# A diffusion layer on one core: gate projections as 32-column strips, context work behind the loop over x

## The chip, the cores and the metric

The kernel runs on one core of one Trainium2 chip. The metric is device microseconds of one execution; the kernel before is given by the median of three runs. A second source is one profiled execution, whose instructions were recorded by the hardware profiler. Its engines are TensorE (PE, with its weight loads shown apart as PEld), VectorE (DVE), ScalarE (ACT), GpSimd (POOL) and SyncE (SP), which issues every DMA of this kernel.

## The reference, cut to what matters

One layer of a diffusion backbone: 512 latent tokens `x` and 256 context tokens `ctx`, both 1024 wide, in fp32.

```
mod  = silu(c) @ w_ada + b_ada            # shift and scale, one value per channel; mod_c the same from c_ctx
h    = rms_norm(x, g)   * (1 + scale)   + shift
hc   = rms_norm(ctx, g) * (1 + scale_c) + shift_c
aq, ak, av, dq, dk, dv, dz, da, db, ga, gd = split(h @ w_in)     # da, db: 16 columns each
caq, cak, ...                              = split(hc @ w_in)
beta = sigmoid(db);  g = -exp(a_log) * softplus(da + dt_bias)    # gates of the delta recurrence
...                                       # attention, delta recurrence, branch projections, MLP
```

The change concerns only the way from `x`, `ctx` and `c` to `h`, `hc`, the first projections (`dk` among them) and the gates `da`, `db`.

## The kernel before

All activations lie channel by channel: the 1024 channels are eight row tiles (`kt`, 0 to 7) of 128 partitions, and tokens are columns, 512 of `x` beside 256 of `ctx`. A projection tile is 128 columns of `w_in`, multiplied for each `kt`. To keep fp32 precision with faster products, weights and activations are split into a high and a low part (`wload`, L240 on ACT for the high part, L241 on DVE for the low one), and `mm3` adds three products for each `kt`: high with high (L289), high with low (L290), low with high (L291). The gates `da` and `db` fill a projection tile of their own, `T_AB`, of whose 128 columns 32 hold weights and the rest zeros.

The start of the kernel, the part that changes, runs as follows.

- 36 products of a constant (L188) run on PE while the first transfers come in.
- The mean square: ACT squares `x` in four pieces (L265), DVE adds the pieces and folds them (L269, L273), one product with a matrix of ones sums over the channels (L276), and ACT takes logarithm and exponential (L146), which gives `rx`. The same follows for the context and gives `rc`.
- Modulation: for each `kt`, `ada(kt)` multiplies the condition vectors with 1 MB of `w_ada`, in two transfers of 512 KB. Its eight products per `kt` (L207) are strips: each writes 32 of the 128 rows of the result, four strips side by side. `columns(kt)` copies the result out (L221, ACT), turns it into columns with two narrow products (L226, PE), and DVE makes the scale column (L229) and the shift column (L230).
- The loop over `kt`: `modulate` gives `h`: DVE multiplies by scale and `rx` (L294), ACT adds the shift and rounds to the high part (L295), DVE forms the low part (L296). It does so for 512 columns of `x` and 256 of the context. `ada` and `columns` of `kt + 2` follow (`AHEAD`), and then `mm3` of three tiles whose weights were loaded early (`EARLY`): `T_AB`, `T_DK` and `T_DK + 1`.
- Then come `T_DK + 2` and `T_DK + 3`, whose weights pass through a queue (`wq`, `wnext`), the gates' element work (L608 to L622), and L649, the first products that use the gates.

Every engine works through its instructions in a fixed order, which the framework's scheduler sets when the program is built, so that the order of the source is not the order of the program: rows of both are shown with the change.

## Time and profile before

| | us |
|---|---|
| median of 3 runs (939.95 to 941.4) | 940.95 |
| span of the profiled execution, first to last instruction | 938.6 |
| PE busy in the span | 907.7 (97%) |
| PE weight loads | 732.9 (78%) |
| DVE busy | 596.5 (64%) |
| ACT busy | 444.2 (47%) |

The span lies 2.35 us under the median of the runs; the profiled execution has no other time of its own. A matmul shows as two entries where its operands are plain fp32. Busy time of PE counts overlapping matmuls once, and the length of a matmul holds its way through the array: matmuls in a dense row follow each other faster than each of them lasts.

### The profile page before, as it was taken

Reading aid. Unit: us, or ns where it says so; the run is one execution under the profiler, and the core shown is the slowest. Engines: PE = TensorE matmul, PEld = TensorE weight load, DVE = VectorE, ACT = ScalarE, POOL = GpSimd, SP = SyncE. Lnnn points to the kernel's source line nnn. Section 1 sums busy time; section 2 is a strip of 40 time slices with the busy share of each in tenths; the row PEclk is TensorE's granted clock in tenths of the full one; section 3 lists DMA queues with packets and bytes.
Section 4 is the critical chain, followed back from the end, with each engine's and each line's share of the span. In section 5 each row is a group of like instructions: output and inputs, shape, how many; then the busy total and the mean of one; then the engine's idle time right before and its main releaser. Section 6 shows DMA issues by size and latency. Waiting matters only on the chain.

```text
span 938.6 us, 18221 instructions
## 1 busy us (share of the span) xinstructions
PE 907.7 (97%) x7768; PEld 732.9 (78%) x7768; DVE 596.5 (64%) x1013; ACT 444.2 (47%) x815; POOL 12.1 (1%) x26
## 2 busy tenths in 40 slices
PE   7999899989899999989999999999999999999998
PEld 5688677867677687778788788988888888888886
DVE  4666789997778898357875877982455235433411
ACT  5467644347567887565555434561243125313400
POOL 0000000000000001100000000000000000000000
PEclk8999999999999999999999999999999999999999
DMA  9911112110000132225424484481344124222111
GB/s 356 361 47 46 47 47 68 46 47 24 23 12 23 34 114 91 93 92 164 153 87 134 146 279 143 140 293 39 101 156 145 47 68 152 95 68 90 46 42 49
DMA packets 29601, 98.73 MB, mean 105 GB/s; under 512 B 3664, under 2 KB 4176, under 8 KB 29520
## 3 DMA queue, kind: packets, MB, share of 16 engines
q1 hardware_dynamic: 29520, 97.57, 31.7%
q8 instruction: 61, 1.00, 0.5%
q14 instruction: 20, 0.16, 0.1%
HBM read 95.46 MB, written 2.10 MB: 104 GB/s over the span
## 4 chain that ended last, share of the span: by engine, by line
PE 70%; DVE 16%; DMA 5%; ACT 5%; issue 3%; SPq 0%; DVEq 0%; ACTq 0%
PE banks L289 15%; PE banks L290 15%; PE banks L291 14%; PE banks L943 10%; DMA wr<-in_wm 2%; DMA wa<-in_wada 2%; DVE wl L241 2%; PE banks L988 2%; PE banks L1054 2%; PE banks L526 1%; DVE m L183 1%; DVE m L773 1%; DVE m L772 1%; PE banks L532 1%; DVE m L1008 1%
## 5 line engine op out<-in xcount | busy, mean ns | idle before, releaser
L289 PE MATMUL banks<-m,m 128*128 128x512 f32 (+1 forms) x584 | 219.5, 379 | 4.5 <-ACT m L240 3.4
L290 PE MATMUL banks<-m,m 128*128 128x512 f32 (+1 forms) x584 | 219.0, 377 | 0.3 <-DVE m L183 0.2
L291 PE MATMUL banks<-m,m 128*128 128x512 f32 (+1 forms) x584 | 218.9, 377 | 0.0
L240 ACT ACTIVATE m<-wr 128x1024 fp32r<-128x1024 f32 x67 | 71.2, 1062 | 158.2 <-PE banks L290 79.6
L289 PEld LDWEIGHTS banks<-m,m 128*128 128x128 f32 x584 | 109.2, 188 | 28.0 <-ACT m L240 3.4
L290 PEld LDWEIGHTS banks<-m,m 128*128 128x128 f32 x584 | 109.5, 188 | 21.9 <-DVE m L241 0.8
L241 DVE TENSOR_TENSOR m<-wr,m 128x1024 fp32r<-128x1024 f32 x67 | 81.9, 1224 | 69.8 <-ACT m L240 40.8
L291 PEld LDWEIGHTS banks<-m,m 128*128 128x128 f32 x584 | 109.3, 188 | 21.4 <-issue 1.2
L289 PE MATMUL banks<-m,wh 128*128 128x512 f32 (+1 forms) x312 | 114.2, 367 | 1.7 <-DVE m L1269 1.0
L291 PE MATMUL banks<-m,wl 128*128 128x512 f32 (+1 forms) x312 | 111.8, 360 | 1.1 <-DVE wl L241 1.1
L290 PE MATMUL banks<-m,wh 128*128 128x512 f32 (+1 forms) x312 | 111.2, 357 | 0.0
L943 PE MATMUL banks<-m,wh 128*128 128x512 f32 x320 | 105.4, 404 | 0.0
L1370 DVE SCALAR_TENSOR_TENSOR m<-banks,modT,m 128x512 f32<-128x512 f32 x32 | 24.0, 750 | 100.9 <-PE banks L291 100.9
L241 DVE TENSOR_TENSOR wl<-wr,wh 128x1024 fp32r<-128x1024 f32 (+1 forms) x60 | 64.7, 1078 | 28.0 <-ACT wh L240 27.7
L240 ACT ACTIVATE wh<-wr 128x1024 fp32r<-128x1024 f32 (+1 forms) x60 | 56.6, 945 | 31.8 <-PE banks L290 16.6
L943 PEld LDWEIGHTS banks<-m,wh 128*128 128x128 f32 x320 | 59.4, 189 | 13.0
L289 PEld LDWEIGHTS banks<-m,wh 128*128 128x128 f32 x312 | 58.9, 189 | 11.7 <-DVE m L1269 1.2
L291 PEld LDWEIGHTS banks<-m,wl 128*128 128x128 f32 x312 | 58.4, 188 | 10.1 <-DVE wl L241 1.6
L943 PE MATMUL banks<-m,wl 128*128 128x512 f32 x160 | 65.6, 410 | 0.0
L290 PEld LDWEIGHTS banks<-m,wh 128*128 128x128 f32 x312 | 58.9, 189 | 8.3 <-issue 0.2
L182 ACT ACTIVATE m<-m 128x512 fp32r<-128x512 f32 (+1 forms) x56 | 35.2, 631 | 49.5 <-DVE m L1353 21.2
L183 DVE TENSOR_TENSOR m<-m,m 128x512 fp32r<-128x512 f32 (+1 forms) x56 | 38.3, 689 | 18.8 <-ACT m L182 18.3
(231 smaller groups left out, 1285.3 us busy)
## 6 DMA issues: line engine op xcount, KB each, us to landing
wr<-in_wm SPq DMA_DIRECT2D x64, 512.0 KB, 3.7
wr<-in_win SPq DMA_DIRECT2D x39, 512.0 KB, 3.7
wa<-in_wada SPq DMA_DIRECT2D x32, 512.0 KB, 4.3
m<-in_wada SPq DMA_DIRECT2D x16, 512.0 KB, 10.2
m<-in_xT SPq DMA_DIRECT2D x8, 512.0 KB, 5.6
wr<-in_wbr SPq DMA_DIRECT2D x16, 256.0 KB, 2.7
wr<-in_wout SPq DMA_DIRECT2D x8, 512.0 KB, 4.3
out<-m SPq DMA_DIRECT2D x8, 256.0 KB, 2.0
```

What stands on the lines that cost most here:

```text
L182: A.activation(r32(hi), src, AF.Copy)
L183: (eng or V).tensor_tensor(r32(lo), src, hi, op=ALU.subtract)
L240: A.activation(r32(hi), raw, AF.Copy)
L241: V.tensor_tensor(r32(lo), raw, hi, op=ALU.subtract)
L289: PE.matmul(acc, w[0][:, k, :], xhi, start=(start and i == 0), stop=False)
L290: PE.matmul(acc, w[0][:, k, :], xlo, start=False, stop=False)
L291: PE.matmul(acc, w[1][:, k, :], xhi, start=False, stop=(stop and i == n - 1))
L526: PE.transpose(pt[:, j * P:(j + 1) * P], probs[j][:, i * P:(i + 1) * P], ident)
L943: PE.matmul(acc.ap, w[x][:, k, :], hx[k][y], start=(k == p == 0), stop=(k == KT - 1 and p == 2))
L988: PE.matmul(pa.ap, w[x][:, j, :], r32(Q[y][:, :, j, :]), start=(j == p == 0), stop=(j == 3 and p == 2))
L1054: PE.matmul(z[r, x * 256 + q * HD:x * 256 + (q + 1) * HD], src[q][r, col(c):col(c) + CH], S[r, q * HD:(q + 1) * HD], start=True, stop=True)
L1370: V.scalar_tensor_tensor(xn_[ct], acc.ap, modT[:, 3, ct:ct + 1], xn_[ct], op0=ALU.mult, op1=ALU.add)
```

## The change

- `T_AB` is gone as a projection tile. Its 32 columns are loaded once (`wab`, 128 KB), and `ab_strips` multiplies them in plain fp32 with the whole `h`, in strips of 32 output rows: four `kt` side by side, twice, and the four strips are added later on DVE. For this ACT writes `h` once more without rounding (L318 for `x`, L337 for the context).
- The squares: each piece is folded to 512 columns and multiplied with the ones at once; the four products add up in PSUM.
- The context's transfer, mean square, modulation and products stand behind the loop over `x`.
- `ada` loads each `kt` in one transfer of 1 MB; 16 warming products stand where 36 stood; the weights of `T_DK + 2` are asked for ahead of the constants.

In the changed kernel L188 is L189, L207 is L209, L221 is L223, L226 is L228, L229 and L230 are L231 and L232, L240 and L241 are L242 and L243, L265 is L264, L276 is L269, L289 to L291 are L297 to L299, L294 to L296 are L302 to L304, L649 is L669.

```diff
-NONES = 36
+CTXAT = 5
+NONES = 16
...
+        wb = alloc(2048)
+        nc.sync.dma_start(out=wb.ap, in_=I["wada1"][kt])
         for half in range(2):
-            wb = alloc(1024)
-            nc.sync.dma_start(out=wb.ap, in_=I["wada1"][kt, half])
...
-    early, EARLY = [], {T_AB: 0, T_DK: 0, T_DK + 1: 0}
+    early, EARLY = [], {T_DK: 0, T_DK + 1: 0}
...
-    columns(0, ada(0))
-    for k4 in range(KT // 4):
-        nc.sync.dma_start(out=cs_[:, k4 * 1024:(k4 + 1) * 1024], in_=I["ctxT"][k4])
-    load_early()
...
+    def rms(src, nt, n, r):
+
+        ss = bank()
         for i in range(nt):
             b = alloc(1024)
             A.activation(b.ap, src[:, i * 1024:(i + 1) * 1024], AF.Square)
-            if tot is None:
-                tot = b
-            else:
-                V.tensor_tensor(tot.ap, tot.ap, b.ap, op=ALU.add)
-                b.free()
...
+            w = 512
+            while w >= n:
+                V.tensor_tensor(b[:, :w], b[:, :w], b[:, w:2 * w], op=ALU.add)
+                w //= 2
+            PE.matmul(ss[:, :n], ones, b[:, :n], start=(i == 0), stop=(i == nt - 1))
+            b.free()
         act(r, ss[:, :n], AF.Ln, bias=epsc, scale=1.0 / D)
         ss.free()
...
+    rms(xs_, 4, SEQ, rx)
+    columns(0, ada(0))
+    wab_ = alloc(256)
+    wab = wab_.ap.rearrange("p (k c) -> p k c", k=KT)
+    nc.sync.dma_start(out=wab_.ap, in_=I["wab"])
+    load_early()
+    ab, tx, tc_ = bank(2), [], []
+
+    def ab_strips(cols, hs, s):
+
+        for g in range(4):
+            m = PE.matmul(ab[32 * g:32 * g + 32, cols], wab[:, 4 * s + g], hs[g][0].ap, start=(s == 0), stop=(s == 1))
+            tc.add_manual_dep(m.ins, hs[3][1].ins.name, nosync, reason="strips together")
+        for _ in range(4):
+            hs.pop(0)[0].free()
...
     for kt in range(KT):
-        t = alloc(768)
...
-        hc.append(modulate(t[:, 512:768], ct_[kt], rc, modA[:, kt, 1:2], modS[:, kt, 1:2],
-                           HCb[:, oc:oc + 256], HCb[:, oc + 256:oc + 512]))
-        t.free()
+        tx.append((t, A.activation(t.ap, t.ap, AF.Identity, bias=modS[:, kt, 0:1])))
         if kt + AHEAD < KT:
             columns(kt + AHEAD, ada(kt + AHEAD))
+        if kt + AHEAD == CTXAT:
+            for k4 in range(KT // 4):
+                nc.sync.dma_start(out=cs_[:, k4 * 1024:(k4 + 1) * 1024], in_=I["ctxT"][k4])
...
-                mm3(acc[:, :512], w, [hx[k]], start=(k == 0), stop=(k == KT - 1), ks=[k])
-                mm3(acc[:, 512:768], w, [hc[k]], start=(k == 0), stop=(k == KT - 1), ks=[k])
...
+                mm3(acc[:, lat_], w, [hx[k]], start=(k == 0), stop=(k == KT - 1), ks=[k])
+        if kt % 4 == 3:
+            ab_strips(lat_, tx, kt // 4)
+    rms(cs_, 2, CTX, rc)
+    for kt in range(KT):
+        t = alloc(256)
+        o = kt * 512
+        hc.append(modulate(t.ap, ct_[kt], rc, modA[:, kt, 1:2], modS[:, kt, 1:2],
+                           HCb[:, o:o + 256], HCb[:, o + 256:o + 512]))
+        tc_.append((t, A.activation(t.ap, t.ap, AF.Identity, bias=modS[:, kt, 1:2])))
+    for (w, acc) in early:
+        mm3(acc[:, ctx_], w, hc)
+    for s in range(2):
+        ab_strips(ctx_, tc_, s)
...
-    acc = in_tile(T_AB, True)
...
-    V.tensor_scalar(ad, acc[0:16, :TOK], dtb[0:16], None, op0=ALU.add)
+    A.activation(ad, ab[0:32, :TOK], AF.Identity, bias=dtb[0:32])
+    for g in range(1, 4):
+        V.tensor_tensor(ad, ad, ab[32 * g:32 * g + 32, :TOK], op=ALU.add)
+    ab.free()
```

The scheduler's order shows at three places what moved. The first is PE in one round of the loop over `kt`. Before, with `m_7` and `m_8` the high and low weights of `T_AB`, `m_22` those of `T_DK`, `m_17` the `x` part of `h` and `m_18` its context part:

```order
L207 MATMUL banks_64<-m_41_352,m_1_117 32x256 [waits DMAHW5_49,DVE_49]
L207 MATMUL banks_64<-m_41_352,m_1_117 32x256 x3
L207 MATMUL banks_64<-m_42_358,m_1_117 32x256 [waits DMAHW6_49]
L207 MATMUL banks_64<-m_42_358,m_1_117 32x256 x3
L289 MATMUL banks_64<-m_17_184,m_7_151 128x512
L290 MATMUL banks_64<-m_17_184,m_7_151 128x512
L291 MATMUL banks_64<-m_17_184,m_8_152 128x512
L226 MATMUL banks_64<-c_prm_67,m_43_364 128x2 [waits Activation_49]
L226 MATMUL banks_64<-c_prm_67,m_43_364 128x2
```

In the changed kernel, with `m_12` and `m_13` the weights of `T_DK`, `m_19` and `m_20` those of `T_DK + 1` and `m_15` the `x` part of `h`:

```order
L209 MATMUL banks_64<-m_29_238,m_1_97 32x256 [waits DMAHW5_49,DVE_49]
L209 MATMUL banks_64<-m_29_238,m_1_97 32x256 x7
L297 MATMUL banks_64<-m_15_155,m_12_149 128x512 [waits Activation_49]
L297 MATMUL banks_64<-m_15_155,m_19_173 128x512
L298 MATMUL banks_64<-m_15_155,m_12_149 128x512 [waits DVE_49]
L228 MATMUL banks_64<-c_prm_67,m_30_248 128x2 [waits Activation_49]
L228 MATMUL banks_64<-c_prm_67,m_30_248 128x2
L299 MATMUL banks_64<-m_15_155,m_13_150 128x512
L298 MATMUL banks_64<-m_15_155,m_19_173 128x512
L299 MATMUL banks_64<-m_15_155,m_20_174 128x512
```

Before, the rows behind L226 go on with fifteen further products of the same round; now the whole round is the ten rows, and L228, which makes the next columns, stands behind the L298 that waits for DVE.

The second place is DVE at the end of the loop over `kt`. Before, each round holds both widths (`m_2` is `x`, `m_3` the context):

```order
L229 TENSOR_SCALAR modA_129<-banks_64,bada1_121,c_prm_67 128x2 [waits PE_49,Activation_49]
L230 TENSOR_SCALAR modS_130<-banks_64,c_prm_67 128x2
L294 SCALAR_TENSOR_TENSOR m_52_474<-m_2_123,modA_129,m_10_157 128x512 [waits DMAHW7_49,DVE_49]
L294 SCALAR_TENSOR_TENSOR m_52_474<-m_3_124,modA_129,m_10_157 128x256
L327 CAST identb_528<-c_ident_524 128x128 [waits DMAHW3_49]
L296 SCALAR_TENSOR_TENSOR m_17_184<-m_52_474,modS_130,m_17_184 128x512 [waits Activation_49]
L296 SCALAR_TENSOR_TENSOR m_18_185<-m_52_474,modS_130,m_18_185 128x256 [waits Activation_49]
```

In the changed kernel the last round of `x` is followed by all of the context (`m_44` to `m_47` are its first four row tiles); four more pairs follow these rows:

```order
L302 SCALAR_TENSOR_TENSOR m_41_358<-m_2_103,modA_109,m_4_111 128x512 [waits DVE_49]
L243 TENSOR_TENSOR wl_54_484<-wr_52_481,wh_53_483 128x1024 [waits DMAHW3_49,Activation_49]
L304 SCALAR_TENSOR_TENSOR m_15_155<-m_41_358,modS_110,m_15_155 128x512 [waits Activation_49]
L302 SCALAR_TENSOR_TENSOR m_44_385<-m_3_104,modA_109,m_4_111 128x256 [waits DMAHW7_49,Activation_49]
L302 SCALAR_TENSOR_TENSOR m_45_390<-m_3_104,modA_109,m_4_111 128x256
L302 SCALAR_TENSOR_TENSOR m_46_395<-m_3_104,modA_109,m_4_111 128x256
L302 SCALAR_TENSOR_TENSOR m_47_400<-m_3_104,modA_109,m_4_111 128x256
L304 SCALAR_TENSOR_TENSOR m_16_156<-m_44_385,modS_110,m_16_156 128x256 [waits Activation_49]
L304 SCALAR_TENSOR_TENSOR m_16_156<-m_45_390,modS_110,m_16_156 128x256 [waits Activation_49]
L304 SCALAR_TENSOR_TENSOR m_16_156<-m_46_395,modS_110,m_16_156 128x256 [waits Activation_49]
L304 SCALAR_TENSOR_TENSOR m_16_156<-m_47_400,modS_110,m_16_156 128x256 [waits Activation_49]
L302 SCALAR_TENSOR_TENSOR m_48_405<-m_3_104,modA_109,m_4_111 128x256 [waits DMAHW0_49]
```

The context's instructions, two in each round before, now stand in one piece behind the last L304, and a split of weights (L243, `wl_54`, for `T_DK + 2`) stands inside the last round.

The third place is DVE where the weights of `T_DK + 3` are split, `wl_77` before:

```order
L296 SCALAR_TENSOR_TENSOR m_18_185<-m_53_499,modS_130,m_18_185 128x256 [waits Activation_49]
L241 TENSOR_TENSOR wl_60_549<-wr_58_546,wh_59_548 128x1024 [waits DMAHW3_49,Activation_49]
L612 TENSOR_SCALAR m_69_566<-banks_64,c_prm_67 16x768 [waits PE_49]
L241 TENSOR_TENSOR wl_77_597<-wr_75_594,wh_76_596 128x1024 [waits DMAHW4_49,Activation_49]
L613 TENSOR_SCALAR m_70_567<-m_69_566 16x768 [waits DVE_49]
L574 SCALAR_TENSOR_TENSOR m_71_578<-banks_64,c_prm_67,m_71_578 128x511 [waits DMAHW0_49,Activation_49]
```

In the changed kernel this split is `wl_75`, in the last row:

```order
L595 SCALAR_TENSOR_TENSOR m_70_538<-banks_64,c_prm_67,m_70_538 128x511 [waits DMAHW2_49,DMAHW1_49,Activation_49]
L595 SCALAR_TENSOR_TENSOR m_69_537<-banks_64,c_prm_67,m_69_537 128x511 [waits Activation_49]
L632 TENSOR_TENSOR m_67_522<-m_67_522,banks_64 32x768 [waits Activation_49]
L596 SCALAR_TENSOR_TENSOR m_69_537<-banks_64,c_prm_67,m_69_537 128x511 [waits DVE_49]
L632 TENSOR_TENSOR m_67_522<-m_67_522,banks_64 32x768 [waits DVE_49]
L595 SCALAR_TENSOR_TENSOR m_69_537<-banks_64,c_prm_67,m_69_537 128x255 [waits Activation_49]
L632 TENSOR_TENSOR m_67_522<-m_67_522,banks_64 32x768 [waits DVE_49]
L596 SCALAR_TENSOR_TENSOR m_69_537<-banks_64,c_prm_67,m_69_537 128x255 [waits DVE_49]
L634 TENSOR_SCALAR m_68_523<-m_67_522 32x768 [waits DVE_49]
L596 SCALAR_TENSOR_TENSOR m_70_538<-banks_64,c_prm_67,m_70_538 128x511
L595 SCALAR_TENSOR_TENSOR m_70_538<-banks_64,c_prm_67,m_70_538 128x255 [waits Activation_49]
L243 TENSOR_TENSOR wl_75_556<-wr_73_553,wh_74_555 128x1024 [waits DMAHW4_49,Activation_49]
```

Before, one instruction on the gates (L612) stands between the end of the loop and the split; now three additions of strips (L632), L634 and seven instructions of the convolution (L595, L596) stand ahead of it.

## Rows read from the trace of the kernel before

**Rows 1.** The page: span, engines (busy us, share, instructions).

```profile
span 938.6 us, 18221 instructions
PE 907.7 (97%) x7768; PEld 732.9 (78%) x7768; DVE 596.5 (64%) x1013; ACT 444.2 (47%) x815; POOL 12.1 (1%) x26
```

**Rows 2.** Windows of the start (us, busy per engine, granted clock, DMA share, GB/s).

```profile
10.00:15.00 5.00, 3.22 (x27) 1.37 (x25) 2.66 (x3) 1.60 (x4) 0.00 (x0) 1.00 1.03 415
15.00:18.00 3.00, 0.61 (x4) 0.52 (x4) 1.66 (x4) 3.00 (x6) 0.00 (x0) 1.00 1.03 411
18.00:25.00 7.00, 5.92 (x21) 1.90 (x21) 3.55 (x5) 1.69 (x4) 0.00 (x0) 0.51 1.03 408
25.00:30.00 5.00, 4.27 (x32) 2.34 (x31) 4.03 (x8) 3.30 (x7) 0.00 (x0) 1.00 1.02 409
30.00:62.00 32.00, 32.00 (x236) 24.69 (x236) 20.86 (x45) 13.35 (x25) 0.61 (x1) 1.00 0.53 193
80.00:98.00 18.00, 18.00 (x239) 14.33 (x238) 11.81 (x22) 12.09 (x21) 0.00 (x0) 1.00 0.10 31
```

**Rows 3.** Timeline, one round of the loop (start, length, engine, line, tiles).

```profile
29.93 0.50 PE L226 MATMUL banks<-c_prm,m 128*128 128x2 f32 x4
...
30.55 0.28 DVE L229 TENSOR_SCALAR modA<-banks,bada,c_prm 128x2 f32<-128x2 f32 x1 [0.53 <-PE banks L226]
...
30.87 0.74 DVE L294 SCALAR_TENSOR_TENSOR m<-m,modA,m 128x512 f32<-128x512 f32 x1
...
31.65 0.73 ACT L295 ACTIVATE m<-m,modS 128x512 fp32r<-128x512 f32 x1 [0.55 <-DVE m L294]
```

**Rows 4.** Timeline of PE, products of both widths, 53 to 55 us.

```profile
53.82 0.40 PE L289 MATMUL banks<-m,m 128*128 128x512 f32 x1
...
54.52 0.28 PE L289 MATMUL banks<-m,m 128*128 128x256 f32 x1
...
54.87 0.40 PE L289 MATMUL banks<-m,m 128*128 128x512 f32 x1
```

**Rows 5.** Timeline of PE, strips of modulation at either clock.

```profile
19.80 1.08 PE L207 MATMUL banks<-m,m 128*32 128x256 f32 x8
...
41.65 1.07 PE L207 MATMUL banks<-m,m 128*32 128x256 f32 x16
```

**Rows 6.** Timeline of PE, the fourth tile begins; the mark.

```profile
62.22 0.87 PE L289 MATMUL banks<-m,wh 128*128 128x512 f32 x2
...
79.35 1.57 PE L649 MATMUL banks<-c_prm,m 64*64 64x16 f32 x48
```

**Rows 7.** Timeline, from the last square of x to the first columns.

```profile
9.62 1.06 ACT L265 ACTIVATE m<-m 128x1024 f32<-128x1024 f32 x1 [0.21 <-DMA m<-in_xT]
...
12.11 0.69 DVE L273 TENSOR_TENSOR m<-m 128x512 f32<-128x512 f32 x1
...
12.95 1.10 PE L276 MATMUL banks<-m,ones 128*128 128x512 f32 x2 [1.29 <-DVE m L273]
...
14.08 0.69 ACT L146 ACTIVATE m<-banks,epsc 128x512 f32<-128x512 f32 x1 [3.40 <-PE banks L276]
...
14.68 0.38 ACT L221 ACTIVATE m<-banks 128x256 f32<-128x256 f32 x1
...
15.12 0.61 PE L226 MATMUL banks<-c_prm,m 128*128 128x2 f32 x4 [0.50 <-ACT m L221]
...
15.91 0.62 ACT L146 ACTIVATE m<-m 128x512 f32<-128x512 f32 x1
```

**Rows 8.** Groups by form, 0 to 80 us (busy us, mean ns).

```profile
L296 DVE SCALAR_TENSOR_TENSOR m<-m,modS,m 128x512 fp32r<-128x512 f32 x8 | 5.9, 734 | 1.5 <-ACT m L295 1.5
...
L296 DVE SCALAR_TENSOR_TENSOR m<-m,modS,m 128x256 fp32r<-128x256 f32 x8 | 3.8, 477 | 0.0
...
L241 DVE TENSOR_TENSOR wl<-wr,wh 128x1024 fp32r<-128x1024 f32 x3 | 3.6, 1214 | 1.7 <-ACT wh L240 1.7
...
L621 DVE TENSOR_TENSOR m<-m,m 16x768 f32<-16x768 f32 x1 | 0.9, 935 | 0.0
```

More of the change, by code (lines that the diff above doesn't have):

```diff
@@ L52 @@
 TABLES = {AF.Ln: [SET_L], AF.Exp: [SET_L, SET_E], AF.Tanh: [SET_E, SET_S], AF.Silu: [SET_S]}
-T_AK, T_AV, T_AQ, T_AB = 0, 1, 2, 6
-T_DK, T_DV, T_DQ, T_DZ = 7, 11, 15, 19
-T_GA, T_GD = 23, 31
-N_IN = 39
+T_AK, T_AV, T_AQ = 0, 1, 2
+T_DK, T_DV, T_DQ, T_DZ = 6, 10, 14, 18
+T_GA, T_GD = 22, 30
+N_IN = 38
 class Buf:
@@ L265, in tile_layer @@
             A.activation(b.ap, src[:, i * 1024:(i + 1) * 1024], AF.Square)
-            if tot is None:
-                tot = b
-            else:
-                V.tensor_tensor(tot.ap, tot.ap, b.ap, op=ALU.add)
-                b.free()
-        w = 512
-        while w >= n:
-            V.tensor_tensor(tot[:, :w], tot[:, :w], tot[:, w:2 * w], op=ALU.add)
-            w //= 2
-        ss = bank()
-        PE.matmul(ss[:, :n], ones, tot[:, :n], start=True, stop=True)
-        tot.free()
+            w = 512
[4 more added lines that the diff above has]
+            b.free()
         act(r, ss[:, :n], AF.Ln, bias=epsc, scale=1.0 / D)
         ss.free()
-    for r in (rx, rc):
         act(r, r, AF.Exp, scale=-0.5)
+    rms(xs_, 4, SEQ, rx)
[11 more added lines that the diff above has]
+            hs.pop(0)[0].free()
     def mm3(acc, w, xs, start=True, stop=True, ks=None):
@@ L317, in tile_layer @@
             for k in range(kt + 1) if kt == k0 else (kt,):
-                mm3(acc[:, :512], w, [hx[k]], start=(k == 0), stop=(k == KT - 1), ks=[k])
-                mm3(acc[:, 512:768], w, [hc[k]], start=(k == 0), stop=(k == KT - 1), ks=[k])
-    for b in ebufs + [xs_, cs_, rstd, scb]:
-        b.free()
+                mm3(acc[:, lat_], w, [hx[k]], start=(k == 0), stop=(k == KT - 1), ks=[k])
[12 more added lines that the diff above has]
+        ab_strips(ctx_, tc_, s)
+    for b in ebufs + [wab_, xs_, cs_, rstd, scb]:
+        b.free()
+    gates = [(T_GD, i) for i in range(ND1)] + [(T_GA, i) for i in range(8)] + [(T_DZ, i) for i in range(4)]
+    gates += [(T_GD, i) for i in range(ND1, 8)]
+    wq = [(I["win"][t], KT) for t in (T_DK + 2, T_DK + 3, T_AK, *range(T_AQ, T_AQ + 4), T_AV, *range(T_DV, T_DV + 4),
+                                      *range(T_DQ, T_DQ + 4), *(t + i for t, i in gates[:ND1]))]
+    wq += [(I["wbr"][0, ct], 4) for ct in range(8)] + [(I["win"][t + i], KT) for t, i in gates[ND1:]]
+    wq += [(I["wbr"][1, ct], 4) for ct in range(8)] + [(I["wout"][ct], KT) for ct in range(8)]
+    wq = [lambda a=a: wload(*a) for a in wq]
+    wn = [wq.pop(0)()]
     ident = cload("ident", [P, P])
@@ L345, in tile_layer @@
         A.activation(trr[:, 2 * n:2 * n + 2], tri[:, 8 * n:8 * n + 2], AF.Copy)
-    gates = [(T_GD, i) for i in range(ND1)] + [(T_GA, i) for i in range(8)] + [(T_DZ, i) for i in range(4)]
-    gates += [(T_GD, i) for i in range(ND1, 8)]
-    wq = [(I["win"][t], KT) for t in (T_DK + 2, T_DK + 3, T_AK, *range(T_AQ, T_AQ + 4), T_AV, *range(T_DV, T_DV + 4),
-                                      *range(T_DQ, T_DQ + 4), *(t + i for t, i in gates[:ND1]))]
-    wq += [(I["wbr"][0, ct], 4) for ct in range(8)] + [(I["win"][t + i], KT) for t, i in gates[ND1:]]
-    wq += [(I["wbr"][1, ct], 4) for ct in range(8)] + [(I["wout"][ct], KT) for ct in range(8)]
-    wq = [lambda a=a: wload(*a) for a in wq]
-    wn = [wq.pop(0)()]
     def wnext():
```

38 lines of the change are left out of this document (18 added, 20 removed).

## The prediction, made before the change was run

> **What bounds the kernel now.** I read the page first: PE is busy for 907.7 of 938.6 us [rows 1], so what counts is PE's time and its gaps. The windows of the start then show where gaps lie: from 30 us on PE is busy 32.00 of 32.00 us and later 18.00 of 18.00, while in 10 to 30 us it waits, and the transfers run at 408 to 415 GB/s without a break [rows 2]. The granted clock is 1.00, its upper level (2.4 GHz), but falls to the lower one (0.51, 1.2 GHz) from 18 to 25 us, after a stretch of 3 us in which PE worked 0.61 us [rows 2]. The timeline gives marks: the fourth projection tile begins at 62.22, and L649 at 79.35 [rows 6]. Behind that mark the order of all engines is the same but for a few places, and PE has no gap until 98 us, so I take a shift of this mark for a shift of the end. All of the change lies ahead of it.
>
> **Why PE is full before.** A round of the loop costs PE nine products of 512 and nine of 256 columns, 0.233 and 0.117 us apart (three of 512 take 0.70 us, three of 256 0.35) [rows 4], thus 3.15 us, eight strips for 1.07 [rows 5], and the two column products for some 0.4: 4.6 us. Against it stands a chain through three engines: from the start of L226 it is 0.62 us to L229, 0.94 to L294, 1.72 to L295, 2.45 to its end [rows 3]; L296 takes 0.73 more [rows 8], and then L290 may run. With hand-overs of 0.05 that is 3.25 us to L290, and 3.5 to the next L226 if that stands right behind. 4.6 us of work hide 3.5 us of chain.
>
> **The change, step by step.** In the changed order a round on PE is six products of 512 (1.4 us), strips and columns, 2.8 us in all, and the next L228 stands behind the L298 that needs DVE's low part. The chain is the longer one now, and rounds take 3.5 us or more; a product after a wait also begins with a weight load of its own, for which I add 0.1 (an estimate; in a dense row it is hidden), so 3.6. I walk to the mark:
>
> Start. The last square of `x` ends at 10.68; a fold of 512 (0.69), one ones product (1.10), logarithm (0.69), exponential (0.62) and L223's copy (0.38) follow [rows 7], with hand-overs the first columns stand at 14.6 instead of 15.1. The three 1024-wide additions are gone; the four ones products but the last lie in the gaps between squares 1.3 us apart. The 20 warming products removed ran ahead of the first strips and cost nothing, unless the clock needs them.
>
> Round 0: 7.5 us. DVE splits the weights of `T_DK` (1.21) [rows 8] between L302 and L304, which puts L298 at 3.8; at the lower clock two products take 0.9 and eight strips 2.1 (four took 1.08) [rows 5]; copy and hand-overs 0.6. Round 1: 5.6, with another split and the strips of column 2 about where the clock rises, at 25 us as before. Rounds 2 and 3: 3.6 each. Round 4: 4.4, set by PE, which has the first four strips of `wab` in it: columns 0.4, the rest of round 3 0.7, these strips 0.9 + 0.9, L209's 1.07, two products 0.5. (A strip of `wab` is 512 columns, twice L207's; four at once by that row are 1.07 us, and the first stands apart in the order.) Round 5: 6.0: in the order the strips and columns of `kt` 6 stand behind all products of round 5, so 0.9 of products, 1.07 of strips and 0.5 of copy join the chain. Round 6: 4.5 and round 7: 4.8, where products and, in 7, the split for `T_DK + 2` (1.21) stand in the chain. Sum 40.0: the loop over `x` ends at 54.6.
>
> Context. Its sixteen DVE instructions come in one piece behind the last L304 (53.6): 16 x 0.48 [rows 8] = 7.7, to 61.3. PE's 48 products need 5.6 us and follow DVE; thirteen (1.5 us) are left at its end, then seven strips (1.0): 64.0. The rest of `T_DK + 2`, 19 products of 512 and 24 of 256, takes 7.2: 71.2. Before, that tile and the next fill 62.22 to 79.35, so it ended at some 70.9. All that PE was spared, the tile `T_AB` (24 x 0.35 = 8.4 us) less 3.8 us of strips, has gone into waiting.
>
> `T_DK + 3`. Its low weights stand on DVE behind the strips' additions and convolutions: from 64.0 two convolution steps (1.5), three additions and L634 (0.94 each by L621) [rows 8], two more steps of 0.74 and three of 0.47, then the split of 1.21: 73.4. L612 before read PSUM in the same way and is no row here, so L621 is the nearest. PE comes to the first low product at 71.9 and waits 1.5. Seven and a third rounds of 1.05 later the mark stands at 81.1, 1.75 later than before. Some further 0.6 us for weight loads after waits in the context makes +2.3 us. The gates are ready by then: from the last addition at 69.4, six ACT steps and two DVE steps of under 1 us, some between convolutions, end near 78.
>
> ACT's sixteen extra passes (L318, L337: 8 x 0.73 + 8 x 0.5 = 9.8 us) lie beside a busy share of 13.35 in 32 us [rows 2] and cost nothing while rounds last 3.6; without that cover the strips would wait for them. The 1 MB transfers cost nothing: at 410 GB/s a column's share needs 2.55 us, less than a round. The weights' own transfer (0.5 MB) and one split that go are hidden before, too.
>
> So 938.6 + 2.3, and with the 2.35 us by which the median lies above the span, **943.3 us**.
>
> **Bounds of what the trace does not show.** The clock is the largest. If it never fell, rounds 0 and 1 would be 1.9 shorter and the sum +0.4; if it rose 3 to 7 us later than before, +1.4 to +2.7 more. The new strips: side by side as L207 (taken), or one after another at the 1.10 of a full 512 product [rows 7], which would add up to 6 us. Restarts after waits: 0 to 1.2 us. That gives 941 to 946.5 as the forecast's own range.
>
> **A rule against the change.** The window 15 to 18 with 0.61 us of work comes ahead of the lower clock, the window 10 to 15 with 3.22 of 5 us does not [rows 2]; a round of 3.6 us with 2.8 of work is nearer to the latter, and I keep 1.00 from 25 us on. The Trainium skill, page "TensorE: Matmul & The Clock Gate", section "Loop structure matters more than you think", warns of loops in which TensorE waits between its tiles, since its clock then drops each time; by it the rounds would run at the lower clock, and the sum would be that of the third rival instead of +2.3. No row here shows a loop of this kind.
>
> **Rivals.**
> First, faster: PE's work stays the bound, as 32.00 of 32.00 says [rows 2]. Then the removed tile counts, -8.4, +3.8 for strips, +0.4 for the context's second ones product, -0.5 at the start: -4.7, 936.3 us. For it speaks that PE is full before; against it the order, with L228 behind L298. It decides where PE's work in a round reaches the chain's 3.5, and that is 0.7 us, one tile's products, away.
> Second, no change: the clock does not fall, because PE's longest gap there is now some 2.2 us (15.0, behind the first columns, to 17.1, where round 0 has its first high part), where before it worked 0.61 in 3 us [rows 2]; the losses then cancel but for 0.4: 941.4 us. Against it: within a further 0.3 us of work PE waits again until 18.4.
> Third, much slower: low clock in the rounds. At half rate PE needs 5.6 us a round, 2 us above the chain; three such rounds are +6, 949 us, all six 955. The strips one after another end there too.
>
> **How the numbers follow.** Forecast 0.55, first rival 0.17, second 0.13, third 0.15. The measurement tells 0.2% (1.9 us) from no change; the forecast's range of +0.4 to +5.6 holds some 0.2 of its 0.55 within that. So slower 0.50, within 0.33, faster 0.17. Range: 937 to 949, which leaves out half of the first and of the third rival.
>
> **What would show it.** Right: strips of column k and k+1 3.5 to 3.7 us apart in rounds 2 to 4, PE waiting for DVE's low part in each; the loop over `x` ending near 55; DVE without a gap for 7.7 us in the context; a wait of PE for `wl` near 72; L669 near 81. Wrong: rounds below 3.2 us (first rival), a clock of 0.5 behind 30 us (third), or an end that moves otherwise than the mark.

## The result, and the profile after

The changed kernel takes **943.88 us** (median of 20 executions, 941.23 to 946.83) against 941.26 us for the kernel before on the same chip (20 executions, 939.44 to 944.11): a ratio of 1.0022, 95% interval 1.0011 to 1.0032. It is slower by 0.2%, about 2.6 us, where 943.3 was forecast. The profiled execution has a span of 940.4 us (938.6 before), and the page's first lines show that PE does less and is not done sooner: 3.1 us less work than in [rows 1], in a span that is 1.8 us longer.

```profile
span 940.4 us, 18120 instructions
PE 904.6 (96%) x7720; PEld 723.9 (77%) x7720; DVE 594.7 (63%) x1014; ACT 451.3 (48%) x831; POOL 12.1 (1%) x26
```

The windows of the start show where (columns as in [rows 2]). Before, PE was busy for all of 30 to 62 us. Now it is idle for 2.92 us of the 20 from 28 to 48, and ahead of the gates the granted clock falls to its lower level three times, in 18 to 21, 25 to 28 and 48 to 55 us. Between these stretches it is at or near 1.00. Before, it fell once there, in 18 to 25 us.

```profile
15.00:18.00 3.00, 0.70 (x3) 0.29 (x2) 2.70 (x5) 1.20 (x2) 0.00 (x0) 0.97 1.02 421
18.00:21.00 3.00, 2.78 (x18) 1.10 (x18) 0.16 (x1) 0.72 (x1) 0.00 (x0) 0.50 1.02 423
21.00:25.00 4.00, 2.24 (x12) 1.23 (x9) 2.48 (x5) 2.05 (x3) 0.00 (x0) 0.93 1.02 424
25.00:28.00 3.00, 3.00 (x20) 1.08 (x20) 0.39 (x1) 0.79 (x2) 0.00 (x0) 0.50 0.99 404
28.00:48.00 20.00, 17.08 (x136) 9.32 (x136) 10.37 (x23) 9.14 (x15) 0.00 (x0) 1.00 0.80 306
48.00:55.00 7.00, 6.42 (x23) 4.49 (x16) 3.46 (x8) 3.38 (x5) 0.73 (x1) 0.54 0.00 1
55.00:83.00 28.00, 27.68 (x182) 22.51 (x183) 20.83 (x38) 23.48 (x41) 0.73 (x1) 0.99 0.13 41
```

One round, in the timeline of all engines, answers to [rows 3]. The reader should follow it as a ring. The columns (L228) run at 28.70 and free DVE's L302 at 29.64. ACT's L303 follows at 30.41, DVE's low part L304 at 31.17, and PE takes the product that waited for it (L298) at 31.97, its weight load (PEld) having waited 0.49 us. Only behind that product stands the next L228, at 32.31. The copy that this L228 reads (L223) had been done since 31.40. The round is 3.61 us long, and the windows count PE busy for 2.99 of it.

```profile
28.70 0.50 PE L228 MATMUL banks<-c_prm,m 128*128 128x2 f32 x4
...
29.64 0.74 DVE L302 SCALAR_TENSOR_TENSOR m<-m,modA,m 128x512 f32<-128x512 f32 x1
...
30.41 0.72 ACT L303 ACTIVATE m<-m,modS 128x512 fp32r<-128x512 f32 x1 [2.10 <-DVE m L302]
...
31.04 0.36 ACT L223 ACTIVATE m<-banks 128x256 f32<-128x256 f32 x1
31.17 0.75 DVE L304 SCALAR_TENSOR_TENSOR m<-m,modS,m 128x512 fp32r<-128x512 f32 x1 [0.79 <-ACT m L303]
...
31.97 0.19 PEld L298 LDWEIGHTS banks<-m,m 128*128 128x128 f32 x1 [0.49 <-DVE m L304]
31.97 0.50 PE L298 MATMUL banks<-m,m 128*128 128x512 f32 x1
...
32.31 0.50 PE L228 MATMUL banks<-c_prm,m 128*128 128x2 f32 x4
...
74.87 0.61 PE L299 MATMUL banks<-m,wl 128*128 128x512 f32 x2 [0.32 <-DVE wl L243]
...
82.76 1.57 PE L669 MATMUL banks<-c_prm,m 64*64 64x16 f32 x48
```

The rows are joined from three stretches of the timeline. The last two are PE's wait for the low weights of `T_DK + 3`, 0.32 us, and the mark (the first product on the gates) at 82.76, which answers to [rows 6]: 3.4 us later than before. The eight sets of columns start at 14.59, 21.81, 28.70, 32.31, 35.91, 40.02, 45.99 and 51.48, and the last product of the loop over `x` ends at 57.7. PE's waits from 14 us to the mark, added up by what ended them (line, releaser, total, times, longest), were 4.5 us before, most of it one wait for the weights' copy, the first row here. Now they are 8.5 us, and most are for ACT's and DVE's steps of a round, as in the four rows behind it:

```profile
PE banks L289 <- ACT m L240: 3.4, 1, 3.4
...
PE banks L297 <- ACT m L303: 4.9, 6, 2.0
PE banks L228 <- ACT m L223: 1.7, 3, 0.7
PE banks L209 <- DVE modS L232: 0.8, 2, 0.6
PE banks L298 <- DVE m L304: 0.5, 1, 0.5
```

### The profile page after: what moved, and what is told of

It reads as the page before. It is cut to its first block, busy times and chain, and to the rows that moved or that the text cites. A ratio compares the mean times of both kernels' runs of the same rounds, so it can differ in the third digit from the quotient of the medians.

```text
span 940.4 us, 18120 instructions
## 1 busy us (share of the span) xinstructions
PE 904.6 (96%) x7720; PEld 723.9 (77%) x7720; DVE 594.7 (63%) x1014; ACT 451.3 (48%) x831; POOL 12.1 (1%) x26
## 4 chain that ended last, share of the span: by engine, by line
PE 75%; DVE 13%; ACT 5%; DMA 3%; issue 2%; SPq 0%; DVEq 0%; ACTq 0%
PE banks L298 16%; PE banks L297 16%; PE banks L299 16%; PE banks L963 10%; DVE wl L243 2%; DMA wa<-in_wada 2%; PE banks L1008 2%; PE banks L1074 2%; PE banks L547 1%; DVE m L793 1%; DVE m L792 1%; PE banks L1105 1%; PE banks L553 1%; PE banks L1086 1%; PE banks L612 1%
## 5 line engine op out<-in xcount | busy, mean ns | idle before, releaser
L297 PE MATMUL banks<-m,m 128*128 128x512 f32 (+1 forms) x568 | 213.5, 381 | 5.6 <-ACT m L303 5.3
L298 PE MATMUL banks<-m,m 128*128 128x512 f32 (+1 forms) x568 | 214.8, 380 | 0.7 <-DVE m L304 0.5
L299 PE MATMUL banks<-m,m 128*128 128x512 f32 (+1 forms) x568 | 214.8, 380 | 0.0
L242 ACT ACTIVATE m<-wr 128x1024 fp32r<-128x1024 f32 x66 | 70.0, 1062 | 158.5 <-PE banks L298 79.9
L297 PEld LDWEIGHTS banks<-m,m 128*128 128x128 f32 x568 | 106.2, 189 | 29.3 <-ACT m L303 7.9
L243 DVE TENSOR_TENSOR m<-wr,m 128x1024 fp32r<-128x1024 f32 x66 | 80.7, 1224 | 70.7 <-ACT m L242 41.6
L298 PEld LDWEIGHTS banks<-m,m 128*128 128x128 f32 x568 | 106.8, 189 | 23.8 <-DVE m L304 3.5
L299 PEld LDWEIGHTS banks<-m,m 128*128 128x128 f32 x568 | 107.0, 189 | 19.6 <-DVE m L243 0.2
L297 PE MATMUL banks<-m,wh 128*128 128x512 f32 (+1 forms) x312 | 114.7, 368 | 1.8 <-DVE m L1289 1.1
L299 PE MATMUL banks<-m,wl 128*128 128x512 f32 (+1 forms) x312 | 112.0, 362 | 2.2 <-DVE wl L243 2.2
L298 PE MATMUL banks<-m,wh 128*128 128x512 f32 (+1 forms) x312 | 111.1, 357 | 0.0
L243 DVE TENSOR_TENSOR wl<-wr,wh 128x1024 fp32r<-128x1024 f32 (+1 forms) x60 | 64.6, 1077 | 26.4 <-ACT wh L242 26.1
L242 ACT ACTIVATE wh<-wr 128x1024 fp32r<-128x1024 f32 (+1 forms) x60 | 56.6, 944 | 31.4 <-PE banks L298 16.3
L297 PEld LDWEIGHTS banks<-m,wh 128*128 128x128 f32 x312 | 58.9, 189 | 11.5 <-DVE m L1289 1.3
L299 PEld LDWEIGHTS banks<-m,wl 128*128 128x128 f32 x312 | 58.3, 188 | 12.1 <-DVE wl L243 3.1
L298 PEld LDWEIGHTS banks<-m,wh 128*128 128x128 f32 x312 | 59.0, 189 | 8.3 <-issue 0.2
```

Of the source, the lines that this page charges most:

```text
L242: A.activation(r32(hi), raw, AF.Copy)
L243: V.tensor_tensor(r32(lo), raw, hi, op=ALU.subtract)
L297: PE.matmul(acc, w[0][:, k, :], xhi, start=(start and i == 0), stop=False)
L298: PE.matmul(acc, w[0][:, k, :], xlo, start=False, stop=False)
L299: PE.matmul(acc, w[1][:, k, :], xhi, start=False, stop=(stop and i == n - 1))
```

## The experiments

Twelve kernels were run. Ratios are to the kernel before on the same chip. The mark is the first product on the gates (L649 before, L669 after), and "behind" is the span less the mark. "Stops" is PE's idle time from 84 to 205 us that the waits put down to no semaphore (the view calls it issue). "At 0.5" is how long the granted clock lies at its lower level behind the mark. The order of PE's instructions behind the mark, as its rows stand in the traces, comes in two kinds: I is the changed kernel's order, or differs from it at 23 places at most; II differs from it at over a hundred, and the kernels of II from ctx_warm's at 18 at most. All times are in us.

| kernel | ratio (95%) | mark | behind | stops | at 0.5 | order |
|---|---|---|---|---|---|---|
| before | 1 | 79.4 | 859.2 | 4.3 | 6.8 | I |
| changed | 1.0022 (1.0011 to 1.0032) | 82.8 | 857.6 | 2.3 | 4.4 | I |
| cols_first | 0.9984 (0.9967 to 1.0) | 82.0 | 858.3 | 4.2 | 5.0 | I |
| cols_strips | 0.9954 (0.9938 to 0.9971) | 77.5 | 856.7 | 4.1 | 3.7 | I |
| warm | 0.9969 (0.9958 to 0.9981) | 77.4 | 859.3 | 4.2 | 3.4 | I |
| warm_first | 1.0004 (0.9982 to 1.0027) | 81.4 | 863.0 | 5.5 | 10.2 | I |
| before_warm | 0.9955 (0.9941 to 0.9969) | 80.4 | 854.4 | 1.4 | 1.1 | I |
| strips_only | 0.9976 (0.9962 to 0.999) | 77.0 | 860.7 | 5.1 | 10.5 | I |
| start_only | 1.0004 (0.9985 to 1.0023) | 78.2 | 860.0 | 4.8 | 3.4 | I |
| copy_first | 0.99 (0.9874 to 0.9925) | 73.5 | 859.2 | 3.3 | 6.8 | I |
| cols_warm | 0.9871 (0.9858 to 0.9883) | 76.2 | 852.2 | 3.8 | 0.0 | II |
| ctx_in_loop | 0.9874 (0.9853 to 0.9894) | 74.3 | 853.7 | 3.5 | 0.3 | II |
| ctx_warm | 0.9843 (0.9831 to 0.9856) | 72.9 | 851.9 | 2.6 | 0.6 | II |
| ctx_shift | 0.9865 (0.9839 to 0.989) | 74.9 | 853.7 | 3.3 | 3.4 | II |

Mark, behind, stops and the clock come from the one profiled execution of each kernel. The table already says that a whole time can't be read for what happened ahead of the mark without the mark beside it: behind the mark, kernels of order I differ by up to 8.6 us, and every kernel of order II is shorter than all of these. Much of this is stops and clock. Taking off the stops, and half of the time at 0.5 (an estimate of what half rate costs while PE is busy), leaves 850.3 to 853.4 us for order I and 848.4 to 850.0 us for order II.

**cols_first: the column products out of the low part's way.**

```diff
 def mm3(acc, w, xs, start=True, stop=True, ks=None, behind=None):
...
-            PE.matmul(acc, w[0][:, k, :], xlo, start=False, stop=False)
+            m = PE.matmul(acc, w[0][:, k, :], xlo, start=False, stop=False)
+            if behind:
+                tc.add_manual_dep(m.ins, behind.ins.name, nosync, reason="columns first")
...
+                    behind=c_last.get(kt + 1))
```

> The changed kernel, but in each round the low-part products (L298) stand behind the two column products of the next column instead of ahead of them; no work is added or removed. Theory A (a chain through DVE, ACT and PE sets the rounds, and it is long because the column products stand behind products that wait for DVE's low part): the column products no longer wait for L304 (0.75 us) and a product, so columns in rounds 2 to 4 come 2.7 to 3.0 us apart instead of 3.6, rounds 0 and 1 get shorter too, the loop over x ends 3 to 5 us earlier than 57.6, and the time falls by 2 to 5 us from the changed kernel's 943.9. Rival B (PE's own work or the transfers set the rounds): 3.6 us stays and the time is within 1 us of 943.9. Rival C (the low clock is what the rounds cost): columns come closer, but stretches at 0.5 grow and less than 1.5 us comes out.

The order was as meant, yet columns in rounds 2 to 4 came 5.7, 5.2 and 4.4 us apart. The windows say why: the clock was at its lower level from 18 to 38 us, though PE was busy for most of that time.

```profile
18.00:25.00 7.00, 6.42 (x31) 3.45 (x27) 2.86 (x5) 3.49 (x5) 0.00 (x0) 0.50 1.01 421
25.00:38.00 13.00, 12.50 (x68) 6.74 (x61) 3.63 (x8) 3.43 (x7) 0.00 (x0) 0.52 0.99 392
```

In the trace it fell at 17.1 and rose at 37.6 us. So this run says nothing on the chain. Stretches at 0.50 grew, as theory C has it, and the mark moved by 0.8 us only; the ratio fell by more than C allowed. Its twelve executions reach from 934.49 us (mean clock 0.996) to 944.45 (0.987).

**cols_strips: the high-part products behind the next strips as well.**

```diff
+            m = PE.matmul(acc, w[0][:, k, :], xhi, start=(start and i == 0), stop=False)
+            if hibehind:
+                tc.add_manual_dep(m.ins, hibehind.ins.name, nosync, reason="strips first")
```

> The kernel of cols_first, and in each round the high-part products (L297) stand behind the strips of the next column as well, which changes the order in rounds 0, 1, 5 and 6 alone. Theory A: the gap of 2.0 us ahead of round 0's first product takes the strips of column 1, and rounds 5 and 6 lose the products that stand ahead of their strips (0.9 us of products and a wait for DVE), so 2 to 4 us less than cols_first. Rival B: the modulation weights of those columns have not landed by then, the strips wait for their transfer, and nothing or less than 0.5 us comes out.

The ratio is 0.003 lower than that of cols_first, 2.8 us, as theory A says. The first gap took the strips of column 1, and PE waited once for a transfer, 1.4 us. The mark moved by 4.5 us, more than expected, because the clock was back at 1.00 for most of 25 to 30 (0.91).

**warm: PE's gaps filled, nothing else changed.**

```diff
+        extra = None
+        for _ in range({0: 8, 1: 4, 5: 4, 6: 3, 7: 3}.get(kt, 0)):
+            prev, extra = extra or c_last[kt], PE.matmul(ab[:, 768:896], ones, ones, start=True, stop=True)
+            tc.add_manual_dep(extra.ins, prev.ins.name, nosync, reason="extra products behind the columns")
```

> The changed kernel with products that nothing reads (ones by ones, 128 columns, into a free part of a bank) in the gaps of PE behind the columns of rounds 0, 1, 5, 6 and 7: 8, 4, 4, 3 and 3 of them, each at most as long as the gap it lies in. Everything else is as it was. Theory A (the granted clock of 0.5 in 18 to 21, 25 to 28 and 48 to 55 us is taken by PE's waits, and costs some 3.5 us there): PE works through the gaps, the clock stays at 1.00 in most of these stretches, and the time falls by 2 to 3.5 us to 940.4 to 942. Rival B (the low clock lies beside waits for the chain anyway, so it costs less than 0.5 us): the time stays within 1 us of 943.9. Rival C: the extra products delay the column products behind them, +1 to +3 us.

Theory A, and by more than it said: the ratio is lower by 0.0053 than the changed kernel's, 5.0 us, and the mark stands 5.4 us earlier, with the order behind it unchanged. The same windows as of the changed kernel, now at 1.00:

```profile
15.00:18.00 3.00, 2.37 (x18) 1.86 (x17) 2.86 (x5) 1.01 (x3) 0.00 (x0) 1.00 1.04 427
18.00:21.00 3.00, 2.50 (x25) 1.48 (x26) 0.13 (x1) 1.90 (x3) 0.00 (x0) 1.00 1.02 423
...
25.00:28.00 3.00, 2.49 (x24) 1.40 (x23) 1.07 (x3) 1.01 (x3) 0.00 (x0) 1.00 0.99 406
...
48.00:55.00 7.00, 7.00 (x45) 5.18 (x45) 6.75 (x16) 5.87 (x14) 1.47 (x2) 1.00 0.23 76
```

Columns start at 14.28, 20.15, 25.58, 29.19, 32.81, 36.91, 42.89 and 47.55. Rounds 2, 3, 4 and 5 (3.61, 3.62, 4.10, 5.98 us) are as long as in the changed kernel, where the clock was at 1.00 as well; rounds 0, 1, 6 and 7 are 1.4, 1.5, 0.8 and 1.4 shorter, and the loop's products end at 52.4. So the chain's rounds stay as they are, and what the clock costs lies on top of them.

**warm_first: the first gap alone.** The edit is warm's with `{0: 8}`.

> The changed kernel with the eight extra products of warm in the first gap alone (14.6 to 17.2 us). Theory A (each fall of the clock comes from the gaps just ahead of it): the clock holds in round 0 and the mark comes 1.3 to 1.5 us earlier than in the changed kernel, the falls near 25 and 48 us stay; 942 to 943. Theory B (the first fall starts the others): the clock stays at 1.00 in round 1 as well, and most of the 4.9 us that warm gains come: 939 to 940.5.

The profile is that of theory A: the mark 1.4 us earlier, the falls near 25 and 48 us still there (0.66 in 25 to 28, 0.55 in 48 to 55). But its executions lie apart: four took 937.87 to 941.14 us at a mean clock of 0.996 to 0.998, eight 944.16 to 946.53 at 0.989 to 0.991; the profiled one is the slowest of all. The same program pays for the lower clock much more in some executions than in others, and the median says little on either theory.

**before_warm: eight extra products in the kernel before,** behind its first columns.

```diff
+        for _ in range({0: 8}.get(kt, 0)):
+            extra = PE.matmul(mp_[:, 128:256], ones, ones, start=True, stop=True)
+            tc.add_manual_dep(extra.ins, prev.ins.name, nosync, reason="extra products behind the columns")
+            prev = extra
```

> The kernel before with eight extra products behind the first columns, in the gap of 3.4 us ahead of its round 0. Theory A (its clock falls at 18 us because of this gap, and the 7 us at 0.51 cost it 1 to 3 us): clock near 1.00 from 18 to 25 us, 939 to 941. Theory B (round 0 waits for the weights and the columns anyway): within 0.7 us of before's 942.

Neither theory holds as put. The clock was 0.81 in 18 to 25 us and 0.58 in 25 to 30: the fall came later instead of not at all, the mark came 1.0 us later, and the span was still 3.8 us shorter. All of that came from behind the mark, where the order is unchanged but PE's stops were 1.4 us instead of 4.3 and the clock was low for 1.1 us instead of 6.8. The median gained 4.3 us; why the eight products should do this so far behind them is not shown.

**strips_only and start_only: one part of the change at a time,** the context left in the loop in both. The first has the strips and their additions alone, with the weights of `T_DK + 2` asked for early as in the changed kernel; the second the sums of squares in PSUM, the 1 MB loads and 16 warming products, with the tile `T_AB` kept.

> The kernel before with the strips for the gates alone: squares of x added on DVE, half loads of the modulation weights, 36 warming products and the context in the loop, all as before. Theory A (the strips carry the gain, which is the tile's 8.4 us less their 3.8 us as far as PE is the bound, and the place of the context behind the loop takes it away again): 3 to 6 us less than before, 936 to 939; what is missing to ctx_in_loop's 929.7 is then the start. Theory B (rounds are bound by the chain here as well, and the tile's products lay in waits): within 2 us of before's 942.

> The kernel before with the new start alone: squares of x and of the context added in PSUM by ones products, whole 1 MB loads of the modulation weights, 16 warming products; the gates' projection tile stays, and the context stays in the loop. Theory A (the start only brings the first columns forward, and what follows is bound by PE): first columns at 14.1 to 14.6 instead of 15.1, time 0 to 1.5 us less than before. Theory B (the start changes when the clock falls and how long): the time moves by more than 2 us in either direction, with the granted clock of 14 to 30 us.

The strips alone move the mark by 2.3 us and the time by 0.24%, between the two theories: PE was busy for all of 25 to 58 us, so what it was spared counts, but the clock was at 0.59 in 18 to 25 and 0.55 in 25 to 30 us, low for 10.2 us instead of 6.8 before. The start alone brings the first columns to 14.28 and the mark 1.1 us forward, and the time stays, as theory A has it.

**ctx_in_loop: the change with the context left where it was.**

```diff
+    rms(cs_, 2, CTX, rc)
...
     for kt in range(KT):
+        hc.append(modulate(t2.ap, ct_[kt], rc, modA[:, kt, 1:2], modS[:, kt, 1:2],
...
+                mm3(acc[:, ctx_], w, [hc[k]], start=(k == 0), stop=(k == KT - 1), ks=[k])
...
+            ab_strips(ctx_, tc_, kt // 4)
...
-    for (w, acc) in early:
-        mm3(acc[:, ctx_], w, hc)
```

> The changed kernel with the context work back inside the loop over x as it was before (its transfer behind the first columns, its sum of squares ahead of the loop, its modulation, products and strips in each round); strips for the gates, sums of squares in PSUM and whole loads stay. Theory A (rounds are bound by the chain, so six products of 256 columns in each, 0.7 us, lie in waits): the loop gets longer by less than the 8.8 us that the context now takes behind it; with two more DVE steps of 0.45 us in a round, rounds of 3.6 to 4.3 us, 2 to 6 us less in all, 938 to 942. Rival B (DVE's and ACT's additional steps stand in the chain in full, 1 us a round or more, and the 1 MB of context ahead of column 1 delays round 0 by 2.5 us): no gain, 943 to 947.

Theory A, by more than it said: 1.5% below the changed kernel. The mark stands 8.4 us earlier than there and 5.0 earlier than before. The windows show PE full again from 30 us on, at 1.00; rounds 2 to 5 take 3.6, 3.9, 4.4 and 4.1 us:

```profile
30.00:46.00 16.00, 15.89 (x142) 10.18 (x134) 9.91 (x23) 9.52 (x19) 0.00 (x0) 1.00 0.31 113
46.00:58.00 12.00, 12.00 (x82) 9.27 (x86) 7.34 (x18) 8.11 (x16) 0.74 (x2) 1.00 0.88 334
```

Round 0 is 9.7 us long, 2.5 more than in the changed kernel, as rival B has it for that round. The other 4.0 us of the 12.4 by which the spans differ come from behind the mark, where the order is now II; they can't be put down to the context's place as such.

**cols_warm and copy_first: the chain at a held clock.** cols_warm has the edits of cols_first and warm together; copy_first adds one on ACT.

```diff
+        if kt + 1 in c_copy:
+            tc.add_manual_dep(tx[-1][1].ins, c_copy[kt + 1].ins.name, nosync, reason="copy first")
```

> Both edits together: the low-part products behind the next column's products (as in cols_first) and the extra products in PE's gaps (as in warm), which take the clock out of the comparison. Theory A (the chain sets the rounds, and the place of the column products makes it 3.6 us): at a clock of 1.00 columns in rounds 2 to 4 come 2.7 to 3.0 us apart instead of warm's 3.6 and the loop over x ends 2 to 4 us earlier than warm's 52.3; the time falls by 2 to 4 us below warm's 939.0, to 935 to 937. Theory B (what cols_first lost was no matter of the clock: PE's own work, or the transfers, hold the rounds): columns still come 3.4 us or more apart, and the time is within 1 us of warm's.

> cols_warm with one more edit of order: on ACT the unrounded pass of a round (L318 of the changed kernel) stands behind the copy of the next column's strips (L223) instead of ahead of it. In cols_warm, at a clock of 1.00, columns came 4.41, 3.17 and 4.43 us apart in rounds 2 to 4; the copy stood behind that pass in the first and the last of these, and ahead of it in the one of 3.17. Theory A (the pass, which has to wait for DVE's low part, has taken the place of the low-part product in the chain): the rounds of 4.4 go to 3.1 to 3.3 (round 4, with the first strips for the gates, to 3.6 to 4.4), the loop over x ends 1.5 to 4 us earlier than cols_warm's 50.7. Theory B (the modulation weights' transfer holds these rounds): they stay at 4.4 on average, whatever ACT's order. The whole time follows the loop's end only as far as the order behind it stays: 926 to 930 by A, 929.9 by B.

In cols_warm the clock is 1.00 throughout, and rounds 2 to 4 take 4.41, 3.17 and 4.43 us. Its timeline, rows of ACT and PE (lines two to six later than in the changed kernel: L309 is its L303, L324 its L318, L225 its L223, L230 its L228): in the first round the copy stands on ACT behind the pass L324, which waits for DVE's low part; in the second it stands ahead of it.

```profile
27.37 0.72 ACT L324 ACTIVATE m<-m,modS 128x512 f32<-128x512 f32 x1 [0.82 <-DVE m L310]
27.99 0.36 ACT L225 ACTIVATE m<-banks 128x256 f32<-128x256 f32 x1
28.41 0.61 PE L230 MATMUL banks<-c_prm,m 128*128 128x2 f32 x4 [1.08 <-ACT m L225]
...
31.12 0.39 ACT L225 ACTIVATE m<-banks 128x256 f32<-128x256 f32 x1 [0.17 <-PE banks L209]
31.58 0.59 PE L230 MATMUL banks<-c_prm,m 128*128 128x2 f32 x4
31.77 0.72 ACT L324 ACTIVATE m<-m,modS 128x512 f32<-128x512 f32 x1 [0.27 <-DVE m L310]
```

With the copy ahead in these rounds (copy_first) round 2 takes 3.16 us, and the mark comes 2.6 us earlier than in cols_warm. Round 3 takes 4.24, because a single gate strip, which costs 1.04 us alone, went ahead of the columns there:

```profile
26.91 0.39 ACT L225 ACTIVATE m<-banks 128x256 f32<-128x256 f32 x1 [0.18 <-PE banks L209]
27.35 0.60 PE L230 MATMUL banks<-c_prm,m 128*128 128x2 f32 x4
...
30.61 1.04 PE L288 MATMUL banks<-m,m 128*32 128x512 f32 x2
...
31.59 0.61 PE L230 MATMUL banks<-c_prm,m 128*128 128x2 f32 x4
```

So neither run did what theory A forecast in full. In cols_warm one round of three came near it (3.17 us for 2.7 to 3.0), and the three together took 12.0 us, more than warm's 11.3. In copy_first round 2 came as forecast and round 4 too (4.0), round 3 did not, and the loop's products end 1.3 us earlier instead of 1.5 to 4. What the two runs show together is the chain: at a clock of 1.00, with the column products and ACT's copy both ahead, a round falls from warm's 3.61 to 3.16 us, and with the copy behind it does not. For the whole time both expectations were off: the span of cols_warm is 8.3 us shorter than warm's, of which 1.2 lie ahead of the mark and 7.1 behind it, where its order is II and its clock never fell; copy_first, with order I and 6.8 us at the lower clock, takes 7.0 us more than cols_warm behind the mark. How much of this is the order alone was not tried.

**ctx_warm and ctx_shift: towards a better kernel.** ctx_warm is ctx_in_loop with 8 and 3 extra products in rounds 0 and 1. ctx_shift does the context of column k in round k + 3 instead, with its sum of squares behind round 2.

> ctx_in_loop with extra products behind the columns of rounds 0 and 1 (8 and 3), where its granted clock is 0.63 to 0.80. Theory A (the low clock costs there too): from 14 to 30 us PE has some 8.5 us of work at the low clock, so the strips and products there take up to 3 us less; 926.5 to 929. Theory B (round 0 is held by the context's sum of squares and its transfer): within 1 us of 929.7.

> A version put together from the runs: the changed kernel with the context's work of column k in round k + 3 of the loop, its load behind column 3's and its sum of squares behind round 2, so that neither stands in round 0, and extra products behind the columns of rounds 0 and 1 (8 and 4). Theory A (ctx_warm's round 0 of 9.7 us is the context's squares on ACT and DVE and its transfer): round 0 takes 5.9 us as in warm, the mark stands 1 to 3 us ahead of ctx_warm's 72.9, and the time is 923 to 926 if the order behind is that of ctx_warm, 927 to 931 if it is that of the changed kernel. Theory B (the work left behind the loop, three columns of the context, costs as much as it saves): 926 to 928 with the same order.

ctx_warm is the best of all, 926.78 us, a ratio of 0.9843 (0.9831 to 0.9856): theory A, with the mark 1.4 us earlier than in ctx_in_loop. It came from round 1, 5.8 us instead of 7.2; round 0 stayed at 9.7, as theory B has it for that round. ctx_shift missed: round 0 took 5.9 us as expected, but the columns of its round 3 came 6.8 us apart, because the strips of that column went behind two rounds' products and the gates' strips. The wait moved, and the mark is 2.0 us later than in ctx_warm.

## Why the prediction was right

The time came within 0.6 us of the forecast, 943.88 for 943.3. The mechanism, waiting in place of PE's work, is shown; that the sum came out so close is in part luck, as its terms say one by one.

**The rounds.** Rounds 2, 3, 4 and 5 were forecast at 3.6, 3.6, 4.4 and 6.0 us and took 3.6, 3.6, 4.1 and 6.0. That the chain is longer than PE's work, and that the place of L228 behind L298 makes it 3.6, is shown: with L228 ahead and ACT's copy ahead of the new pass, at the same clock, a round takes 3.16 (copy_first). "Cost nothing" fits ACT's passes in rounds 2 to 5 of the changed kernel's own order; with L228 moved ahead (cols_warm) they stand in the chain. The sign named for the rounds, a wait for DVE's low part, shows in rounds 2 and 3 at the weight load of L298 (0.49 us each, with PE itself still counted busy); in round 4 it does not.

**The first columns** stood at 14.59 (14.6), and the four strips of `wab` took 1.07 us together, as taken from [rows 5].

**The clock: the right mechanism, too small.** The sum took the lower clock as in [rows 2], to 25 us and not after, worth 1.9 us, and named "a clock of 0.5 behind 30 us" as the sign of the third rival. It fell again in 25 to 28 and 48 to 55 us. Round 1 took 6.9 us instead of 5.6, round 6 5.5 instead of 4.5, round 7 6.2 instead of 4.8, and the loop ended at 57.7 instead of 54.6. Held at 1.00 (warm), the mark is 5.4 us earlier, 0.3 of it ahead of the first extra product, so the term is some 5 us and not 1.9. The mechanism of the third rival is there, in a part of the loop and not in the even rounds of 3.6 us. The Trainium skill, page "TensorE: Matmul & The Clock Gate", section "Loop structure matters more than you think", warns of a loop with a long wait for a transfer ahead of each tile. The trace shows falls with other and shorter waits, for ACT and DVE and of 2.0 us at most, around rounds 0, 1, 6 and 7; rounds 2 to 4 stay at 1.00 with waits of their own, so the rounds as a whole did not run at the lower clock.

**Behind the loop: too long by 1.5 us,** or 2.1 with the restarts. From the loop's end to the mark 26.5 us were forecast, 25.0 were needed, in warm too. The sixteen DVE steps of the context took 6.4 us and not 7.7 (0.40 each in a row), and the first products of `T_DK + 2` ran at 54.4 already, ahead of the context. The wait for `wl` came at 74.6, 0.32 us long instead of 1.5.

**The mark and the end.** "A shift of this mark for a shift of the end" is the step that failed. The mark moved by 3.4 us, the span by 1.8, so the changed kernel took 1.6 us less behind the mark. Its stops there are 2.0 us shorter and its clock is low for 2.4 us less, some 1.2 us by the estimate of half rate; the rest is 1.6 us longer. Ten profiles with order I lie between 854.4 and 863.0 us behind the mark, so the way behind it can't be taken as fixed. The sum for the mark was 1.1 us too small (+2.3 for +3.4), because the clock's term was short by more than the way behind the loop was too long. The end followed by less, +1.8 us in the two profiled executions and +2.6 in the medians. The errors met: the forecast owes its closeness of 0.6 us in part to that. Two of its own signs of being wrong did appear, the clock at 0.54 in 48 to 55 us and an end that moved otherwise than the mark.

**The first rival** (PE's work stays the bound, -4.7 us) needed PE's work of a round to reach the chain's. With the context in the loop it does, and the mark is 5.0 us earlier than before (start_only's 1.1 among them). The rival's -4.7 is near to that, for another place of the context; that its terms are what makes up the 5.0 us is not shown, as the clock was low for 10.2 us there. Moving the context behind the loop then costs the mark 8.4 us, clock included. The second rival needed the clock not to fall. With the clock held (warm) the change came out below before, 0.9969, and not at no change.

## What to carry to other kernels

Work taken from an engine counts only while that engine is the bound: before removing it, add up what the other engines' chain needs in the same round, and keep filling work (here the context's products) where it hides that chain. Here some gaps on TensorE cost twice, the wait and then a stretch at the lower clock, so products that nothing reads paid for themselves in gaps that could not be closed (warm, 5.0 us). Where a scheduler sets the order, compare marks along the program too: here edits at the start reordered what lies far behind them, and the kernels with the new order took 851.9 to 853.7 us behind the mark, the others 854.4 to 863.0. Look there for stops and for the clock before the order gets the credit.
